# Moving every large on-chip tile of a hybrid decoder layer to a multiple of 512 bytes

## The chip, the core and the metric

The kernel runs on one core of one Trainium2 chip. Time is device time in microseconds (us) of one execution of the whole layer. The kernel before takes 894.34 us, the median of three runs (893.3 to 895.06).

## What is computed

One layer of a decoder trunk, 512 tokens of 1024 channels, in float32. The input is normed and projected (`z = u @ w_in`) into the inputs of three mixers: a chunked gated linear attention of 4 heads, a short gated convolution, and a sliding-window attention of 8 query and 2 key heads with sinks. Each mixer's output is projected back, the three are weighted by sigmoid gates and summed, and go through `w_o` into the residual. Then a second norm, a gated MLP, and a last norm:

```python
z = rmsnorm(h, g_mix) @ w_in                       # 1024 -> 7440 columns
merged = (gt[..., :D] * (o_gla @ w_gla_o) + gt[..., D:2*D] * (y_conv @ w_conv_o)
          + gt[..., 2*D:] * (o_swa @ w_swa_o))
h = h + merged @ w_o
hid = causal_dwconv(rmsnorm(h, g_ffn) @ w_up, ffn_conv_w)
h = h + (silu(hid[..., :2816]) * hid[..., 2816:]) @ w_down
out = rmsnorm(h, g_final)
```

## The kernel before

**Products.** Every large product is exact to about float32: each factor is split into two float32r parts, hi and lo, and three products are summed in one bank of PSUM: hi by hi, hi by lo, lo by hi. `by_channel` (line 173) holds a tile of weights still (128 columns of `whi` or `wlo`) and streams 512 tokens of an activation (`uh`, `ul`, or the outputs of the mixers) past it; its products are line 177. `by_token` (line 181) does the reverse: it holds 128 tokens of an activation still and streams 512 columns of weights past them; its products are lines 183, 184 and 186. Each product loads its still operand anew (PEld in the profile); the product itself (PE) is 512 columns wide, or 256 in two places where only half of the tokens are ready.

**Stages.** Input norm and first queries (to about 22 us), queries, keys, gates and the factors of the linear attention (to about 100 us), values, window attention and convolution (to about 245 us), the output gate `gr`, by `by_token`, the branch gates `gt` and output projections `ya`, `yb` of the three mixers, by `by_channel` (to about 470 us), the output projection `wo`, by `by_token` (to about 515 us), the MLP's up projection `ug`, `uu`, by `by_channel` (to about 764 us), and its down projection `wd`, by `by_token` (to the end).

**Side work.** The class `W` (line 52) streams weight blocks: while the products of one block run, ScalarE and VectorE split the next (lines 91 and 92), and SyncE loads the one after it (line 68). The small stages of the mixers are generators in a list `side`; `tick()` (line 107) takes one step of each after every 12 products. A scheduler then orders each engine's instructions. None of this is touched by the change.

**Where tiles lie.** A tile takes the same bytes of all 128 partitions. Pools are laid one behind the other from the low end in the order in which they are opened, or from the high end where `side="right"` is given; each tile is rounded up to 32 bytes. Line 43 opens `pc` (constants), line 44 `pw` (the weight blocks: three `raw`, two `whi`, two `wlo`, 8192 bytes each), line 45 `ph` (the four residual tiles `h`, 4096 bytes each), line 47 `small` (four of each of some thirty tiles of 4 to 32 bytes). `pU` (`uh` and `ul`, 16384 bytes each, later `uh2` and `ul2` in the same place) is opened behind `small`. The 45 slots of 2048 bytes (`pS`, line 249) grow from the high end, and after the output projection `pF` takes their place there (`xh`, `xl`, `yg`, `yu`, `p`). The constants end at byte 23840, which is 288 past a multiple of 512, so that the weight blocks and `h` lie 288 past one; the small tiles then put `uh` and `ul` at 416 past one; and the slots, counted from the high end, at 480 past one. All three are 32 past a multiple of 64. Tiles within a pool are multiples of 512 bytes apart, and the pieces of them that products read start at multiples of 512 bytes within the tile.

Of the kernel before, what the change touches and what calls it, by code (L numbers as in the profile page):

```python
# [7 lines left out]
F32 = mybir.dt.float32  # L8
# [6 lines left out]
P = 128  # L15
# [8 lines left out]
EPS = 1e-6  # L24
TAU = 16.0
NCONST = 6 * P
NSLOT = 45  # scratch tiles of [128, 512] up to the output projection
HEAD_STEPS = 3  # steps from the start of one linear-attention head to that of the next
LAG_STEPS = 5  # steps that a head's products wait for their factors
WINDOW_STEPS = 5  # steps from one window's start to the next one's  # L30

GQ, GK, GV, GR, GA = 0, 512, 1024, 1536, 2048
CX, CB, CC = 2064, 2576, 3088
# [4 lines left out]
def trunk(ctx, tc, x, g_mix, w_in, w_alpha, b_alpha, norm_g, conv_w, sinks, w_gla, w_conv, w_swa,  # L38
# [2 lines left out]
    mm = nc.tensor.matmul  # L41

    pc = ctx.enter_context(tc.tile_pool(name="pc", bufs=1))
    pw = ctx.enter_context(tc.tile_pool(name="pw", bufs=2))
    ph = ctx.enter_context(tc.tile_pool(name="ph", bufs=1))
    ps = ctx.enter_context(tc.tile_pool(name="ps", bufs=8, space=bass.MemoryType.PSUM))
    small = ctx.enter_context(tc.tile_pool(name="small", bufs=4))

    def bank():
        return ps.tile([P, 512], F32, tag="b", name="bank")  # L50

    class W:
        """A stream of weight blocks of 2048 columns per partition, each split exactly into two
        float32r parts. While the products of block i run, block i + 1 is split, in pieces, and
        block i + 2 is loaded."""

        def __init__(self):
            self.todo, self.raw, self.done, self.pieces = [], [], [], []
# [45 lines left out]
    at = {}  # L104
    side = []

    def tick():
        """One step of whatever runs beside the large products."""
        w.piece()
        for task in list(side):  # L110
            if next(task, side) is side:
                side.remove(task)
# [29 lines left out]
    for j in range(4):  # L142
        for b in range(3):
# [14 lines left out]
            n=1024,  # L158
# [32 lines left out]
        nc.vector.tensor_sub(out=lo, in0=src, in1=hi.bitcast(F32))  # L191

    def rstd_of(ss, n, tag, log=False):
        """(ss / n + EPS) ** -0.5, refined by one Newton step."""
        shape = list(ss.shape)
        v = small.tile(shape, F32, tag=tag + "v", name="v")
        r = small.tile(shape, F32, tag=tag + "r", name="r")
        t = small.tile(shape, F32, tag=tag + "t", name="t")
        nc.vector.tensor_scalar(out=v, in0=ss, scalar1=1.0 / n, scalar2=EPS, op0=ALU.mult, op1=ALU.add)
        if log:  # L200
            nc.scalar.activation(out=t, in_=v, func=AF.Ln)
            nc.scalar.activation(out=r, in_=t, func=AF.Exp, scale=-0.5)
        else:
            nc.scalar.activation(out=t, in_=v, func=AF.Sqrt)
            nc.vector.reciprocal(out=r, in_=t)
        u = small.tile(shape, F32, tag=tag + "u", name="u")
        nc.vector.tensor_mul(out=u, in0=r, in1=r)
        nc.vector.tensor_mul(out=u, in0=u, in1=v)
        nc.vector.tensor_scalar(out=u, in0=u, scalar1=-0.5, scalar2=1.5, op0=ALU.mult, op1=ALU.add)
        nc.vector.tensor_mul(out=r, in0=r, in1=u)  # L210
        return r

    def rstd_1(ss, e, n, tag, log=False):
        """(ss / n + e[0]) ** -0.5 for one column, refined by one Newton step; e[1] is -e[0] / 2."""
        v = small.tile([P, 1], F32, tag=tag + "v", name="v")
        r = small.tile([P, 1], F32, tag=tag + "r", name="r")
        t = small.tile([P, 1], F32, tag=tag + "t", name="t")
        if log:
            nc.scalar.activation(out=t, in_=ss, func=AF.Ln, scale=1.0 / n, bias=e[0])
            rstd_1.last = nc.scalar.activation(out=r, in_=t, func=AF.Exp, scale=-0.5)  # L220
        else:
            nc.scalar.activation(out=t, in_=ss, func=AF.Sqrt, scale=1.0 / n, bias=e[0])
            nc.vector.reciprocal(out=r, in_=t)
        nc.vector.tensor_scalar(out=v, in0=ss, scalar1=-0.5 / n, scalar2=e[1], op0=ALU.mult, op1=ALU.add)
        nc.vector.tensor_scalar(out=v, in0=v, scalar1=r, scalar2=r, op0=ALU.mult, op1=ALU.mult)
        nc.vector.tensor_scalar(out=r, in0=v, scalar1=1.5, scalar2=r, op0=ALU.add, op1=ALU.mult)
        return r

    def rstd_part(ss, n, tag, engine=nc.vector):
        """The first part of a sum of squares, for rstd_1 of the rest."""  # L230
        e = small.tile([P, 2], F32, tag=tag + "e", name="e")
        engine.tensor_scalar(out=e[:, 0:1], in0=ss, scalar1=1.0 / n, scalar2=EPS, op0=ALU.mult, op1=ALU.add)
        engine.tensor_scalar_mul(e[:, 1:2], e[:, 0:1], -0.5)
        return e[:, 0:1], e[:, 1:2]

    # ---- the input and its norm
    zero = pc.tile([P, 256], F32, name="zero")
    nc.vector.memset(zero, 0.0)
    idle = bank()

    def warm(n):
        """Products of zeros, to hold the tensor engine's clock up until the input is there."""
        for _ in range(n):
            mm(idle[:, 0:256], zero[:, 0:P], zero, start=True, stop=True)

# [78 lines left out]
        return ul[:, k, :]  # L324

    def a_tile(name, j, n=slice(0, S), acc=None):
        """Tile j of the channels of a weight block, by token."""
        if name == "gq0":
            hi, lo = (a.rearrange("p (j k c) -> p j k c", j=2, c=P)[:, j] for a in w.take(at[name]))
        else:  # L330
            hi, lo = (a.rearrange("p (k j c) -> p j k c", j=2, c=P)[:, j] for a in w.take(at[name]))
        acc = acc or bank()
        by_channel(acc, lambda k: hi[:, k], lambda k: lo[:, k], uhk, ulk, n=n)
        return acc

    def b_tiles(name):
        """The four token tiles of 512 channels, each as it is ready."""
        accs = [bank() for _ in range(NT)]
        for i in range(2):
            hi, lo = (a.rearrange("p (k c) -> p k c", c=512) for a in w.take(at[f"{name}{i}"]))  # L340
            for t in range(NT):
                tok = slice(t * P, (t + 1) * P)
                by_token(accs[t], lambda k: uh[:, 4 * i + k, tok], lambda k: ul[:, 4 * i + k, tok],
                         lambda k: hi[:, k, :], lambda k: lo[:, k, :], 4, i == 0, i == 1)
                if i:
                    yield t, accs[t]

    # ---- linear attention: queries, keys and gates
    qs, ks = [None] * GH, [None] * GH

    def got_q(h, acc):
# [78 lines left out]
            la[h] = z  # L430

    def running_sums(y, n):
        """In place: the sums of the first 1, 2, .. n of every n columns."""
        s = 1
        while s < n:
            g = y.rearrange("p (g s) -> p g s", s=2 * s)
            nc.vector.tensor_add(out=g[:, :, 2 * s - 1], in0=g[:, :, 2 * s - 1], in1=g[:, :, s - 1])  # L437
            s *= 2
        s = n // 4
        while s:  # L440
            g = y.rearrange("p (n g s) -> p n g s", s=2 * s, g=n // (2 * s))
            nc.vector.tensor_add(out=g[:, :, 1:, s - 1], in0=g[:, :, 1:, s - 1], in1=g[:, :, :-1, 2 * s - 1])
            s //= 2

    # ---- linear attention: the factors of each head
    ATs, qIs, kTs, decs = [None] * GH, [None] * GH, [None] * GH, [None] * GH

    def factors(h):
# [89 lines left out]
        nc.scalar.copy(out=v, in_=acc)  # L538
        vs.append(v)

    # ---- linear attention: states and outputs
    Os = [None] * NT

    def normed(n, O):
# [44 lines left out]

    side.append(states())  # L590

    # ---- window attention
    lower, upper = slice(0, 64), slice(64, 128)
    sqs = []
    for t in range(4):
# [36 lines left out]
    def window(n):  # L632
# [15 lines left out]
            return sps  # L648

        def biased(pr, sps):  # L650
            """Each query's last 128 keys: those of its own block up to itself, the others of the block before."""
            for i in range(2):
                s = slot(name="sc")[:, 0:256].rearrange("p (g j) -> p g j", g=2)
                ps2 = sps[i].rearrange("p (g j) -> p g j", g=2)
# [48 lines left out]
        for kt in kts:  # L703
            for g in range(2):
                t = n - 1 + kt
                mm(ops[64 * g:64 * g + 64, :], sv[:, t * P + 64 * g:t * P + 64 * g + 64], pts[kt, g],  # L706
                   start=kt == kts[0], stop=kt == 1)
# [10 lines left out]
    side.append(values())  # L718
    side.append(windows())

    # ---- short convolution
    def conv3(acc, cwj, name):
        """Three causal taps over the tokens, from PSUM or SBUF."""
        y = slot2(name=name)
        nc.scalar.activation(out=y, in_=acc, func=AF.Copy, scale=cw[:, 2, cwj:cwj + 1])  # L725
        nc.vector.scalar_tensor_tensor(out=y[:, 1:], in0=acc[:, :S - 1], scalar=cw[:, 1, cwj:cwj + 1],  # L726
# [24 lines left out]
            och.append(hi)  # L751
            ocl.append(lo)

    # ---- linear attention: output gate
    ogh = [slot(F32R, name="ogh") for _ in range(4)]
    ogl = [slot(F32R, name="ogl") for _ in range(4)]

# [15 lines left out]
    for t, acc in b_tiles("gr"):  # L773
        side.append(gated(t, acc))

    # ---- the gated sum of the branches
    mh, ml = [], []
    for j in range(4):
        gts = []
# [29 lines left out]
    uh = pU.tile([P, KT, S], F32R, name="uh2")  # L809
    ul = pU.tile([P, KT, S], F32R, name="ul2")  # L810

    # ---- output projection, residual, norm
    gf = [slot(name="gf") for _ in range(2)]
    for i in range(2):
        nc.gpsimd.dma_start(out=gf[i], in_=g_ffn[None, 512 * i:512 * i + 512].to_broadcast([P, 512]))
# [47 lines left out]
                elif two:  # L863
                    h_split(t - 2, hn[t - 2])

    # ---- gated MLP with a convolution
    first3 = [("ug0", 0), ("ug0", 1), ("uu0", 0)]
    early = []
    for i, (name, j) in enumerate(first3):
# [19 lines left out]
    xs = [None] * len(DOWN)  # L889

    def split_prods(i):
        """The factors of block i, split a tile at each step."""
        k0, kt = DOWN[i]
        xs[i] = [[], []]
        for k in range(kt):
            for part, name in zip(xs[i], ("xh", "xl")):
                part.append(pF.tile([P, 512], F32R, tag="t", name=name, bufs=22))
            split(xs[i][0][k], xs[i][1][k], prods[k0 + k])
            yield
# [92 lines left out]
```

## Time and profile before

| | |
|---|---|
| median of the runs (lowest, highest) | 894.34 us (893.3, 895.06) |
| profiled execution, span from first to last instruction | 891.6 us |
| PE busy, share of the span, instructions | 879.0 us, 99%, 3976 |
| PEld busy | 705.9 us, 79%, 3976 |
| DVE busy | 475.2 us, 53%, 822 |
| ACT busy | 342.8 us, 38%, 607 |
| POOL busy | 59.1 us, 7%, 58 |
| DMA | 82.39 MB, mean 92 GB/s |

PE is TensorE's products, PEld its loads of the still operand, DVE is VectorE, ACT ScalarE, POOL GpSimd, SP SyncE. Products are pipelined, so that the busy time of one (some 390 ns) is longer than the time from its start to the next one's start, and a PE busy at 99% isn't yet PE at its peak. What tells its rate is how many products start in a stretch of time. [...] What lies outside the span makes the difference between 891.6 and 894.34 us.

### The profile page before, as it was taken

Reading aid. Unit: us, or ns where it says so; the run is one execution under the profiler, and the core shown is the slowest. Engines: PE = TensorE matmul, PEld = TensorE weight load, DVE = VectorE, ACT = ScalarE, POOL = GpSimd, SP = SyncE. Lnnn points to the kernel's source line nnn. Section 1 sums busy time; section 2 is a strip of 40 time slices with the busy share of each in tenths; the row PEclk is TensorE's granted clock in tenths of the full one; section 3 lists DMA queues with packets and bytes.
Section 4 is the critical chain, followed back from the end, with each engine's and each line's share of the span. In section 5 each row is a group of like instructions: output and inputs, shape, how many; then the busy total and the mean of one; then the engine's idle time right before and its main releaser. Section 6 shows DMA issues by size and latency. Waiting matters only on the chain.

```text
span 891.6 us, 10006 instructions
## 1 busy us (share of the span) xinstructions
PE 879.0 (99%) x3976; PEld 705.9 (79%) x3976; DVE 475.2 (53%) x822; ACT 342.8 (38%) x607; POOL 59.1 (7%) x58
## 2 busy tenths in 40 slices
PE   8999999999999999999999999999999999999996
PEld 6887887767678888888888898888888888888885
DVE  5599566765633251526234666555555555743734
ACT  6545543443434132322223444333333333532533
POOL 2027003000000000101010000000000000001100
PEclk9999999999999999999999999999999999999999
DMA  9431331211222333233325134222222223222202
GB/s 278 145 94 48 95 95 48 86 56 48 78 66 71 95 93 115 77 95 96 87 79 165 48 118 139 93 92 93 94 92 93 92 69 113 96 71 95 95 1 94
DMA packets 69862, 82.39 MB, mean 92 GB/s; under 512 B 2875, under 2 KB 58455, under 8 KB 69815
## 3 DMA queue, kind: packets, MB, share of 16 engines
q1 hardware_dynamic: 69511, 80.70, 28.4%
q0 software_dynamic: 304, 1.05, 0.4%
q8 instruction: 31, 0.51, 0.2%
q14 instruction: 16, 0.13, 0.0%
HBM read 79.64 MB, written 2.10 MB: 92 GB/s over the span
## 4 chain that ended last, share of the span: by engine, by line
PE 92%; DVE 4%; ACT 1%; POOL 1%; issue 0%; DMA 0%; ACTq 0%
PE bank L177 64%; PE bank L184 7%; PE bank L183 7%; PE bank L186 7%; PE bank L647 1%; PE bank L706 1%; PE bank L646 1%; DVE wlo L92 1%; POOL d L461 1%; DVE z L437 1%; DVE d L479 0%; PE bank L693 0%; PE bank L566 0%; DMA h<-in_x 0%; ACT xsq L299 0%
## 5 line engine op out<-in xcount | busy, mean ns | idle before, releaser
L177 PE MATMUL bank<-uh,whi 128*128 128x512 f32 (+1 forms) x792 | 302.7, 386 | 1.9 <-ACT uh L315 1.6
L177 PE MATMUL bank<-ul,whi 128*128 128x512 f32 (+1 forms) x792 | 303.1, 386 | 0.2
L92 DVE TENSOR_TENSOR wlo<-raw,whi 128x1024 fp32r<-128x1024 f32 x144 | 176.5, 1259 | 196.1 <-ACT whi L91 113.0
L91 ACT CAST whi<-raw 128x1024 fp32r<-128x1024 f32 x144 | 144.4, 1048 | 174.6 <-PE bank L177 145.8
L177 PE MATMUL bank<-uh,wlo 128*128 128x512 f32 (+1 forms) x792 | 192.8, 384 | 0.0
L177 PEld LDWEIGHTS bank<-uh,whi 128*128 128x128 f32 x792 | 149.4, 189 | 35.5 <-ACT uh L315 2.1
L177 PEld LDWEIGHTS bank<-ul,whi 128*128 128x128 f32 x792 | 149.8, 189 | 33.4 <-issue 0.8
L177 PEld LDWEIGHTS bank<-uh,wlo 128*128 128x128 f32 x792 | 144.0, 188 | 32.3 <-issue 0.8
L184 PE MATMUL bank<-whi,xl 128*128 128x512 f32 x176 | 68.8, 392 | 0.0
L183 PE MATMUL bank<-whi,xh 128*128 128x512 f32 x176 | 67.9, 391 | 0.0
L186 PE MATMUL bank<-wlo,xh 128*128 128x512 f32 x176 | 48.0, 391 | 0.0
L191 DVE TENSOR_TENSOR xl<-p,xh 128x512 fp32r<-128x512 f32 x44 | 30.2, 726 | 26.9 <-ACT xh L190 22.6
L183 PEld LDWEIGHTS bank<-whi,xh 128*128 128x128 f32 x176 | 33.1, 188 | 7.3
L186 PEld LDWEIGHTS bank<-wlo,xh 128*128 128x128 f32 x176 | 33.1, 188 | 7.2
L184 PEld LDWEIGHTS bank<-whi,xl 128*128 128x128 f32 x176 | 33.1, 188 | 7.1
L190 ACT CAST xh<-p 128x512 fp32r<-128x512 f32 x44 | 24.7, 616 | 36.3 <-PE bank L184 36.3
L725 ACT ACTIVATE yg<-bank,cw 128x512 f32<-128x512 f32 x22 | 15.1, 685 | 53.3 <-PE bank L177 53.3
L797 DVE TENSOR_TENSOR g<-bank,g 128x512 f32<-128x512 f32 x24 | 16.5, 689 | 32.0 <-PE bank L177 31.4
L800 POOL TENSOR_TENSOR g<-g 128x512 f32<-128x512 f32 x8 | 13.4, 1673 | 302.7 <-DVE g L797 300.7
L784 ACT ACTIVATE g<-bank 128x512 f32<-128x512 f32 x24 | 14.3, 596 | 48.2 <-PE bank L177 48.1
L907 ACT ACTIVATE yg<-yg 128x512 f32<-128x512 f32 x22 | 13.9, 631 | 47.9 <-DVE yg L728 47.9
L726 DVE SCALAR_TENSOR_TENSOR yu<-bank,cw,yu 128x511 f32<-128x511 f32 x22 | 16.4, 747 | 26.4 <-ACT yu L725 26.4
(211 smaller groups left out, 963.1 us busy)
## 6 DMA issues: line engine op xcount, KB each, us to landing
raw<-in_w_in SPq DMA_DIRECT2D x28, 1024.0 KB, 5.2
raw<-in_w_up SPq DMA_DIRECT2D x22, 1024.0 KB, 5.1
raw<-in_w_down SPq DMA_DIRECT2D x10, 1024.0 KB, 5.0
raw<-in_w_o SPq DMA_DIRECT2D x4, 1024.0 KB, 5.0
h<-in_x SPq DMA_DIRECT2D x4, 512.0 KB, 4.8
raw<-in_w_gla_o SPq DMA_DIRECT2D x4, 512.0 KB, 3.4
raw<-in_w_conv_o SPq DMA_DIRECT2D x4, 512.0 KB, 4.6
raw<-in_w_swa_o SPq DMA_DIRECT2D x8, 256.0 KB, 4.1
```

The source lines that it names most:

```text
L91: nc.scalar.copy(out=hi[:, c], in_=raw[:, c])
L92: nc.vector.tensor_sub(out=lo[:, c], in0=raw[:, c], in1=hi[:, c].bitcast(F32))
L177: mm(acc[:, n], a, b[:, n], start=i == 0, stop=i == len(todo) - 1)
L183: mm(acc, xh(k), hi(k), start=start and k == 0, stop=False)
L184: mm(acc, xl(k), hi(k), start=False, stop=False)
L186: mm(acc, xh(k), lo(k), start=False, stop=stop and k == kt - 1)
L190: nc.scalar.copy(out=hi, in_=src)
L191: nc.vector.tensor_sub(out=lo, in0=src, in1=hi.bitcast(F32))
L725: nc.scalar.activation(out=y, in_=acc, func=AF.Copy, scale=cw[:, 2, cwj:cwj + 1])
L726: nc.vector.scalar_tensor_tensor(out=y[:, 1:], in0=acc[:, :S - 1], scalar=cw[:, 1, cwj:cwj + 1], in1=y[:, 1:], op0=ALU.mult, op1=ALU.add)
L784: nc.scalar.activation(out=g, in_=acc, func=AF.Sigmoid)
L797: nc.vector.tensor_mul(out=g, in0=acc, in1=g)
```

## The change

The pool of small tiles is opened directly behind the constants, ahead of the weight blocks, and is followed by a padding tile of 96 bytes; at the high end a padding tile of 480 bytes is laid first. Comments and docstrings fall away, and six lines are added ahead of most of the code, so that a line of the kernel after has the number of the line before plus 6 (line 177 becomes 183).

```diff
+PAD_LEFT, PAD_RIGHT = 96, 480
...
     pc = ctx.enter_context(tc.tile_pool(name="pc", bufs=1))
+    small = ctx.enter_context(tc.tile_pool(name="small", bufs=4))
+
+    pad = ctx.enter_context(tc.tile_pool(name="pad", bufs=1))
+    pad.tile([P, PAD_LEFT // 4], F32, name="pad")
+    pad_r = ctx.enter_context(tc.tile_pool(name="pad_r", bufs=1, side="right"))
+    pad_r.tile([P, PAD_RIGHT // 4], F32, name="pad_r")
     pw = ctx.enter_context(tc.tile_pool(name="pw", bufs=2))
     ph = ctx.enter_context(tc.tile_pool(name="ph", bufs=1))
     ps = ctx.enter_context(tc.tile_pool(name="ps", bufs=8, space=bass.MemoryType.PSUM))
-    small = ctx.enter_context(tc.tile_pool(name="small", bufs=4))
```

In the built programs every engine has the same instructions in the same order, with the same shapes and the same waits, and each tile name falls on the same buffer of its pool. What differs is the first byte of the tiles:

| tiles | first byte before | past a multiple of 512 | first byte after | past a multiple of 512 |
|---|---|---|---|---|
| constants (`zero`, `cst`, `rows`, ...) | 16512 | 128 | 16512 | 128 |
| `small` | 97568 | 288 | 23840 | 288 |
| `raw`, `whi`, `wlo` | 23840 | 288 | 27136 | 0 |
| `h` | 81184 | 288 | 84480 | 0 |
| `uh`, `uh2` / `ul`, `ul2` | 100768 / 117152 | 416 | 100864 / 117248 | 0 |
| slots of `pS` and `pF` | 137184 | 480 | 136704 | 0 |

## Rows read from the trace of the kernel before

**Rows 1.** Busy time, share of the span and instructions, by engine

```profile
PE 879.0 (99%) x3976; PEld 705.9 (79%) x3976; DVE 475.2 (53%) x822; ACT 342.8 (38%) x607; POOL 59.1 (7%) x58
```

**Rows 2.** Chain that ended last: shares by engine

```profile
PE 92%; DVE 4%; ACT 1%; POOL 1%; issue 0%; DMA 0%; ACTq 0%
```

**Rows 3.** PE's own waits: us in total, times, longest us

```profile
PE bank L177 <- ACT uh L315: 1.6, 2, 1.4
PE bank L244 <- DVE zero L238: 1.2, 1, 1.2
```

**Rows 4.** Stretches: PE, PEld, DVE, ACT, POOL busy (x instructions), PEclk, DMA share, GB/s

```profile
251.00:265.00 14.00, 14.00 (x62) 11.37 (x61) 6.45 (x8) 5.08 (x6) 0.00 (x0) 1.00 0.24 76
320.00:348.00 28.00, 28.00 (x122) 22.74 (x121) 7.33 (x8) 7.39 (x10) 0.00 (x0) 1.00 0.34 102
470.00:505.00 35.00, 35.00 (x154) 28.73 (x154) 15.78 (x32) 10.96 (x21) 0.00 (x0) 1.00 0.38 126
540.00:760.00 220.00, 220.00 (x944) 177.02 (x943) 117.99 (x140) 76.36 (x100) 0.00 (x0) 1.00 0.28 94
768.00:882.00 114.00, 114.00 (x500) 93.58 (x499) 58.69 (x86) 45.63 (x72) 6.18 (x4) 1.00 0.22 78
```

**Rows 5.** PE in order of time: start us, us, engine line op tiles shapes

```profile
14.31 0.42 PE L177 MATMUL bank<-uh,whi 128*128 128x256 f32 x1
...
15.16 0.41 PE L177 MATMUL bank<-uh,whi 128*128 128x256 f32 x1
17.88 0.28 PE L177 MATMUL bank<-uh,whi 128*128 128x256 f32 x1
...
19.80 1.12 PE L177 MATMUL bank<-uh,wlo 128*128 128x256 f32 x8
```

**Rows 6.** The same view of three early stretches

```profile
14.20:15.40 1.20, 1.20 (x8) 1.20 (x8) 1.20 (x4) 1.20 (x6) 0.47 (x2) 0.50 1.19 169
17.80:20.70 2.90, 2.90 (x27) 2.90 (x26) 1.21 (x4) 0.00 (x0) 0.00 (x0) 1.00 1.05 339
22.00:100.00 78.00, 76.94 (x383) 62.41 (x384) 61.98 (x126) 42.88 (x82) 23.69 (x15) 1.00 0.31 96
```

**Rows 7.** Groups by line and shape: count, busy us, mean ns, idle before

```profile
L177 PE MATMUL bank<-uh,whi 128*128 128x512 f32 x712 | 282.4, 397 | 0.0
L184 PE MATMUL bank<-whi,xl 128*128 128x512 f32 x176 | 68.8, 392 | 0.0
L183 PE MATMUL bank<-whi,mh 128*128 128x512 f32 x64 | 25.3, 395 | 0.0
L177 PE MATMUL bank<-osh,whi 128*128 128x512 f32 x32 | 12.7, 396 | 0.0
L177 PE MATMUL bank<-ul,whi 128*128 128x256 f32 x80 | 21.0, 301 | 0.2
L177 PEld LDWEIGHTS bank<-ul,whi 128*128 128x128 f32 x792 | 149.8, 189 | 33.4 <-issue 0.8 <-DVE ul L316 0.8 <-DVE ul L191 0.2
```

**Rows 8.** Line 177 by stretch: PE busy (x), PEld busy (x), PEclk, DMA

```profile
100.00:250.00 150.00, 103.00 (x419) 76.85 (x417) 1.00 0.23 71
250.00:480.00 230.00, 202.03 (x864) 162.29 (x864) 1.00 0.31 94
525.00:764.00 239.00, 238.43 (x1056) 193.08 (x1056) 1.00 0.28 93
```

**Rows 9.** VectorE groups by line and shape

```profile
L728 DVE SCALAR_TENSOR_TENSOR yg<-bank,cw,yg 128x510 f32<-128x510 f32 x22 | 16.5, 749 | 0.7
L726 DVE SCALAR_TENSOR_TENSOR yg<-bank,cw,yg 128x511 f32<-128x511 f32 x22 | 16.4, 747 | 21.3 <-ACT yg L725 21.3
L828 DVE SCALAR_TENSOR_TENSOR hn<-h,r,gf 128x512 f32<-128x512 f32 x8 | 5.7, 748 | 0.1
```

**Rows 10.** Chain in order of time, its only DMA: start us, us, what

```profile
0.72 3.25 DMA h<-in_x
```

**Rows 11.** DMA issues: count, KB each, median us to landing

```profile
raw<-in_w_up SPq DMA_DIRECT2D x22, 1024.0 KB, 5.1
```

## The prediction, made before the kernel after was run

> **What bounds the kernel now.** I read the busy times first, then the chain, PE's waits, and last how many products start in a stretch. PE is busy 99% of the span while DVE has 53% and ACT 38% [rows 1], and the chain that ended last lies on PE for 92% [rows 2]; its longest waits are 1.6 and 1.2 us [rows 3]. So the time is the number of products times the time from one start to the next, plus some 22 us ahead and 7 us behind. Nothing is issued, waited for or loaded differently after the change. It can act only by making some access to on-chip memory faster or slower, and on PE that counts at once.
>
> The interval is found from a stretch with nothing else on PE. A product shows for 0.39 us [rows 7], so the products that touch a stretch of L us cover L + 0.39 us of starts. The up projection: 220.39 / 944 = 233.5 ns. The branch gates: 28.39 / 122 = 232.7. The output gate: 14.39 / 62 = 232.1. The output projection: 35.39 / 154 = 229.8. The down projection: 114.39 / 500 = 228.8 [rows 4]. One product too many or few makes 3.7 ns at the output gate, 1.5 at the output projection, 0.5 or less in the two longest. All have 512 columns, a fresh load of 128 columns and the full clock. The output gate and the two later `by_token` stages run the same code; they differ in the tile that is held still, which lies at 416 past a multiple of 512 in the first and at 480 in the others. Nor do the other engines explain it: DVE is busy 54% of the up and 51% of the down projection, DMA 28% and 22%, ACT 35% and 40% [rows 4], too alike for two rates. So the rate seems to hang on where the operands lie. This is the only sign in the trace that the change can do anything.
>
> How large can it be? At the half clock, 0.50 granted, four products of 256 columns take 15.16 - 14.31 = 0.85 us, 212.5 each [rows 5, 6]; by the ratio of the clocks 512 columns take 212.5 at the full one. There the interval is 228.8 to 233.5, so 16.3 to 21 ns of each are not columns. At the full clock 16 products of 256 columns take 19.80 - 17.88 = 1.92 us, 120.0 each [rows 5], against 233.1 (mean of gates and up projection) for 512 columns with the same tiles. If an interval is a fixed part and a part that grows with columns, the fixed part is 2 x 120.0 - 233.1 = 6.9 ns and the other 113.1 per 256 columns, some 6.9 above the bare columns.
>
> **The change part by part.** *Products.* Before, every operand of the long products begins 32 bytes past a multiple of 64. My estimate is that the fixed 6.9 ns is what an operand pays that begins inside a unit of the memory, one unit more than it fills; 6.9 ns is about the time of 16 columns (212.5 / 512 x 16 = 6.6), 64 bytes, which fits a start in the middle of such a unit. It is only an estimate: no warm product of the trace has both operands on a multiple of 64. With the tiles at 0 it goes, and the part that grows with columns stays. The count from 250 us on, where PE never idles: 864 of line 177 up to 480 us, 984 in the up projection (1,056 less 72 of 256 columns) [rows 8], 192 of the output projection, 528 of the down projection (three times 64 and 176) [rows 7], and some 66 of the output gate (to 265 us at 232 ns), 2,634 in all: x 6.9 = 18.2 us. The 144 short ones around 515 to 535 us give 1.0. Between 100 and 250 us 419 of line 177 [rows 8] and some 30 of the output gate run beside the attention's side work; I count half, 1.5 us. Before 100 us I count none: DVE is busy 61.98 of 78 us there [rows 6] and its results come late as it is. Sum 20.7 us: 891.6 - 20.7 = 870.9 in the profiled execution, and with the 2.7 us that the median lies above that span, 874 us.
>
> Bounds for one product: if the whole gap goes, 16.3 ns for the 720 of output and down projection and 20.6 for the other 2,616 of the 3,336 long ones (712, 176, 64 and 32 of each kind in rows 7, with their fellows), that is 11.7 + 53.9 = 65.6 us, down to 829. On the other side, the new position can cost one more such fixed part, 3,336 x 6.9 = 23 us, up to 917. I take the middle of the gain, since the fixed part is the row nearest to what a shift of the start can change.
>
> Against this speaks the half clock: the same tiles in the same place show no gap there at all, so the start inside a unit is not a cost that every product pays, only perhaps one that becomes visible when columns are taken twice as fast. [...]
>
> *Loads of the still operand.* They take 189 ns [rows 7] beside a product whose interval is 229 or more, and are hidden by it; only where they slow the product's own reading do they count, and that is in the intervals above.
>
> *VectorE and ScalarE.* Of the same operation, 512 elements from a tile's start take 748 ns, 511 from 4 bytes later 747, 510 from 8 bytes later 749 [rows 9]: the place costs nothing. From -2 to 2 ns on some 1,400 instructions off the path: 0.
>
> *DMA.* The chain holds one transfer, 3.25 us for the first rows of the input [rows 10]; the weight blocks land in 5.1 us [rows 11], and the 48 products of one in the up projection take 48 x 233.5 ns = 11.2 us. A fifth more or less on the first transfer would be 0.65 us either way; I take 0.
>
> *Padding tiles, small tiles.* No instruction touches the padding. The small tiles keep their residue of 288. 0.
>
> **The rivals.** *Nothing happens.* The difference between stages comes from which region or pair of tiles is read, not from the residue; these stay as they are, and the time stays 894.3 (892.5 to 896.1). For it: no gap at the half clock, VectorE's indifference. Against it: `by_token` at 232.1 and 228.8 with one code.
>
> *Slower: the two readers of TensorE collide.* Before, the streamed and the held operand never have the same residue (288 with 416, 480, or the reverse). After, both begin at 0. The best pair, streamed 288 and held 480, gives 228.8; the others some 233. If equal residues are like the worse pairs, output and down projection lose 233.5 - 228.8 = 4.7 ns on 720 products, 3.4 us, and the rest stays: 897.7. The end is 917 as above. It decides if starts in the down projection come no closer than 233 ns.
>
> *Small gain.* Only the pair matters, and equal residues are as good as the best one seen: 2,616 products gain 233.1 - 228.8 = 4.3, 11.2 us: 883.
>
> *Large gain.* More than half of the whole gap goes: below 862, with the end at 829. [...]
>
> **How the numbers follow.** Forecast (862 to 884) 0.34; large gain 0.08; small gain (884 to 892.5) 0.10; nothing 0.29; slower 0.19. A time within 0.2% of before, 892.5 to 896.1, is what a measurement of this kernel can't tell from no change. Faster is 0.34 + 0.08 + 0.10 = 0.52, same 0.29, slower 0.19. The range for 8 in 10 must reach from part of the large gain over no change to the small loss: 852 to 898, which leaves out some 0.05 below and 0.10 above. Cases of both signs hold much of this; the forecast's own range is 862 to 884.
>
> **What would show it.** In the profile after, the up projection's stretch should hold 220.39 / 0.2266 = 973 products instead of 944, the down projection's 114.39 / 0.2219 = 515 instead of 500, at the same clock; the product's own shown duration should shrink by about as much. The durations of VectorE and ScalarE groups and the landings of loads should stay within 1%. PE's waits before 100 us may grow by 1 to 2 us. I am wrong if the intervals stay (nothing happens), if only the former 233 ns stages move (the pair matters, not the start), if the down projection slows, or if the time moves while the intervals of the long products don't.

## The result, and the profile after

The changed kernel takes 877.77 us (median of 4 runs, 877.42 to 878.00) beside 894.00 us of the kernel before on the same chip (893.30 to 895.06): a ratio of 0.982, interval 0.981 to 0.983. The profiled execution took 878.0 us, its span 876.2. The forecast was 874 us. The direction and most of the size came out; the reason that I gave for them did not, and that is what the experiments are about.

TensorE (PE) is still what bounds the kernel. The page's busy times, the answer to [rows 1]:

```profile
PE 862.9 (98%) x3976; PEld 705.2 (80%) x3976; DVE 474.2 (54%) x822; ACT 343.2 (39%) x607; POOL 59.4 (7%) x58
```

The counts are those of before. PE lost 16.1 us of busy time; the loads, VectorE and ScalarE kept theirs to 1 us. So the instructions of one engine became shorter, and that engine is the path.

Four stretches of the kernel after, in the columns of [rows 4] (branch gates, output projection, up and down projection; all stages begin earlier now, so the stretches differ a little):

```profile
320.00:348.00 28.00, 28.00 (x126) 23.18 (x125) 5.63 (x5) 8.27 (x11) 0.00 (x0) 1.00 0.29 92
462.00:497.00 35.00, 35.00 (x156) 29.01 (x155) 16.13 (x31) 11.64 (x22) 0.00 (x0) 1.00 0.40 133
540.00:760.00 220.00, 220.00 (x973) 182.15 (x972) 123.89 (x148) 85.40 (x114) 0.00 (x0) 1.00 0.28 94
768.00:860.00 92.00, 92.00 (x408) 76.18 (x407) 43.96 (x64) 35.32 (x56) 6.16 (x4) 1.00 0.19 63
```

By the same count of starts, (length + 0.39) / products: branch gates 28.39 / 126 = 225.3 ns (one product more or less is 1.8), output projection 35.39 / 156 = 226.9, up 220.39 / 973 = 226.5, down 92.39 / 408 = 226.4. Before they were 232.7, 229.8, 233.5 and 228.8. The two rates have become one, at the same granted clock (PEclk, a share of full speed) of 1.00. (The last 49 products in the up projection's stretch and the last 6 in that of the branch gates belong already to the stage behind.) Counted from start to start inside the output gate, it is 226.7 (below). A product's shown duration fell less, from 397 to 393 ns for `uh` with `whi` and from 392 to 389 for `whi` with `xl` (before in [rows 7]). The output gate, PE in order of time (start, length, line, operation, output <- streamed, held, shapes):

```profile
255.10 0.39 PE L189 MATMUL bank<-whi,uh 128*128 128x512 f32 x1
...
257.82 0.39 PE L189 MATMUL bank<-whi,uh 128*128 128x512 f32 x1
```

From 255.10 to 257.82 lie 12 starts: 2.72 / 12 = 226.7 ns.

The short products did not gain. The same 16 starts as in [rows 5], of 256 columns at the full clock:

```profile
18.03 0.28 PE L183 MATMUL bank<-uh,whi 128*128 128x256 f32 x1
...
19.95 1.12 PE L183 MATMUL bank<-uh,wlo 128*128 128x256 f32 x8
```

19.95 - 18.03 = 1.92 us, 120.0 ns each, what they took before. The 144 short ones between the output and the up projection even lost. The same 48 of them, in the kernel before (first two lines) and after:

```profile
526.31 0.28 PE L177 MATMUL bank<-uh,whi 128*128 128x256 f32 x1
...
532.01 0.28 PE L177 MATMUL bank<-uh,whi 128*128 128x256 f32 x1
518.59 0.28 PE L183 MATMUL bank<-uh,whi 128*128 128x256 f32 x1
...
524.35 0.28 PE L183 MATMUL bank<-uh,whi 128*128 128x256 f32 x1
```

5.70 / 48 = 118.8 ns before, 5.76 / 48 = 120.0 after.

What else the change could have touched stayed: VectorE's groups, the answer to [rows 9], each within 1 ns:

```profile
L734 DVE SCALAR_TENSOR_TENSOR yg<-bank,cw,yg 128x510 f32<-128x510 f32 x22 | 16.5, 748 | 0.7
...
L732 DVE SCALAR_TENSOR_TENSOR yg<-bank,cw,yg 128x511 f32<-128x511 f32 x22 | 16.4, 747 | 19.7 <-ACT yg L731 19.7
```

The chain's only transfer, the answer to [rows 10] (3.25 us there):

```profile
0.72 3.37 DMA h<-in_x
```

And the weight blocks of the up projection, with the median time to landing last, the answer to [rows 11] (5.1 us there):

```profile
raw<-in_w_up SPq DMA_DIRECT2D x22, 1024.0 KB, 5.0
```

PE's own longest waits (us in total, times, longest), with [rows 3]:

```profile
PE bank L183 <- ACT uh L321: 1.6, 2, 1.4
PE bank L315 <- DVE xn L309: 1.2, 2, 0.6
```

The first is as before; the transposes' waits for `xn` summed to 1.1 us before, so nothing new stands on the path.

Where the 15.4 us of the span came from, by the start of the first product of each stage in the two traces:

| stage (first product to the next stage's) | before, us | after, us | change | forecast |
|---|---|---|---|---|
| up to the output gate | 238.50 | 236.67 | -1.83 | -1.5 |
| output gate, branch gates, branch outputs | 229.92 | 224.41 | -5.51 | -6.4 |
| output projection | 38.48 | 38.08 | -0.40 | -1.3 |
| transposes and short products | 17.47 | 17.50 | +0.03 | -1.0 |
| up projection | 238.90 | 232.45 | -6.45 | -6.8 |
| down projection | 120.64 | 119.46 | -1.18 | -3.6 |
| after the last product | 7.69 | 7.65 | -0.04 | 0 |

The output projection's row ends with the first transposes of the second norm: its last 24 products lie in the row below, and half of the 144 short products in that of the up projection. The forecast's column is its own count of products times 6.9 ns. It holds where the interval was 233 ns, is three times too large where it was 229, and has the wrong sign for the short products.

### The profile page after: what moved, and what is told of

It is laid out like the page before. It is cut to its first block, busy times and chain, and to the rows that moved or that the text cites. A ratio compares the mean times of both kernels' runs of the same rounds, so it can differ in the third digit from the quotient of the medians.

```text
span 876.2 us, 10006 instructions
## 1 busy us (share of the span) xinstructions
PE 862.9 (98%) x3976; PEld 705.2 (80%) x3976; DVE 474.2 (54%) x822; ACT 343.2 (39%) x607; POOL 59.4 (7%) x58
## 4 chain that ended last, share of the span: by engine, by line
PE 92%; DVE 4%; ACT 1%; POOL 1%; issue 0%; DMA 0%; ACTq 0%
PE bank L183 64%; PE bank L190 7%; PE bank L189 7%; PE bank L192 7%; PE bank L653 1%; PE bank L712 1%; PE bank L652 1%; DVE wlo L98 1%; POOL d L467 1%; DVE z L443 1%; DVE d L485 0%; PE bank L699 0%; PE bank L572 0%; DMA h<-in_x 0%; ACT xsq L305 0%
## 5 line engine op out<-in xcount | busy, mean ns | idle before, releaser
L183 PE MATMUL bank<-ul,whi 128*128 128x512 f32 (+1 forms) x792 | 298.7, 381 | 0.2
L183 PE MATMUL bank<-uh,wlo 128*128 128x512 f32 (+1 forms) x792 | 188.9, 379 | 0.0
```

The source lines that it names most:

```text
L183: mm(acc[:, n], a, b[:, n], start=i == 0, stop=i == len(todo) - 1)
```

## The experiments

The theories, with the letters that the expectations use. **A**, the one of the prediction: an operand pays that begins inside a 64-byte unit. **B**: what counts is how far the start of the streamed operand lies from that of the held one; where they are equal in the low part of the address, a product takes least. **B1** is B with a repetition after 256 bytes, which the second bench tests. **C**: only multiples of 512 bytes, or of some other number above 64, help. Of these, only B lets two tiles at a "bad" place run fast.

**All tiles at 64, and all at 32.** Two kernels, the changed one with other sizes of the two padding tiles.

```diff
-PAD_LEFT, PAD_RIGHT = 96, 480
+PAD_LEFT, PAD_RIGHT = 160, 416    # all tiles 64 past a multiple of 512
+PAD_LEFT, PAD_RIGHT = 128, 448    # all tiles 32 past a multiple of 512
```

> The kernel after with both padding tiles changed (160 and 416 bytes), so that every large tile lies 64 past a multiple of 512. Theory A (an operand that starts off a multiple of 64 bytes costs a unit): as after, 877.8 us, up and down projection at 226.7 ns. Theory B (equal residues of streamed and held operand are what helps): also 877.8. Theory C (only multiples of 512, or of some number above 64, help): up projection back at 230 to 234 ns, 885 to 895 us.

> The kernel after with padding tiles of 128 and 448 bytes: every large tile lies 32 past a multiple of 512, so all residues are equal and none is a multiple of 64. Theory A: the gain goes, 890 to 897 us, intervals 229 to 234 ns. Theory B: the gain stays, 877.8 us, 226.7 ns. Theory C: as A.

At 64: 877.71 us, ratio 0.983 (0.982 to 0.984). At 32: 878.58 us, 0.984 (0.983 to 0.986). Up and down projection of the kernel with all tiles at 32, in the columns of the stretches above:

```profile
540.00:760.00 220.00, 220.00 (x973) 182.21 (x972) 124.57 (x150) 85.24 (x113) 0.00 (x0) 1.00 0.29 94
768.00:860.00 92.00, 92.00 (x408) 76.20 (x407) 43.76 (x64) 35.98 (x58) 6.16 (x4) 1.00 0.19 63
```

The same counts as after, 973 and 408, though every operand now begins inside a 64-byte unit as before. A falls, and C with it: that a tile lies at a multiple of 512 brings nothing by itself.

**Before, everything 32 bytes further on.** The converse: all operands at multiples of 64 (streamed and held at 320, 448 and 0 past a multiple of 512), their differences as before.

```diff
+    pad.tile([P, 8], F32, name="pad")        # ahead of pw
+    pad_r.tile([P, 120], F32, name="pad_r")  # right side
```

> The kernel before with a tile of 32 bytes ahead of the weight blocks and one of 480 at the high end: weight blocks at 320, uh and ul at 448, slots at 0, so that every pair of residues differs by as much as before (the differences -128, 128, 192) but all are multiples of 64. Theory A: 877.8 us and 226.7 ns in every stage. Theory B: as before, 894 us, 233 ns in the up and 229 in the down projection. Theory C: 885 to 894 us.

893.29 us, ratio 1.000 (0.999 to 1.001). Up and down projection:

```profile
540.00:760.00 220.00, 220.00 (x944) 176.98 (x943) 117.68 (x139) 77.08 (x100) 0.00 (x0) 1.00 0.29 94
768.00:882.00 114.00, 114.00 (x500) 93.54 (x499) 58.99 (x86) 45.70 (x73) 6.17 (x4) 1.00 0.23 79
```

944 and 500 products, to the unit what [rows 4] hold. Moving both operands together changes nothing at either place.

**Products alone, by place.** Groups of 48 products of 512 columns, a fresh load each, other engines idle, at chosen places of the streamed and the held operand (bytes past a multiple of 512).

```
tiles "sa".. streamed, "ha".. held; per pair 48 times:
nc.tensor.matmul(acc, tiles[held], tiles[streamed], start=..., stop=...)
```

> Products alone: 48 of 512 columns for each of 20 pairs of places of a streamed and a held operand, and of 256 columns for four pairs; the rest of the layer is left out and the output holds the input. Theory A: 226.7 ns where both operands start at a multiple of 64, whatever their difference; 229 to 234 where one or both start 32 past one; more for the streamed operand than for the held one, since the held one's load has 40 ns to spare. Theory B: 226.7 where the residues are equal, also at 32 and 32. Theory C: 226.7 at 0 and 0 alone. At 256 columns 120 ns at every place, as in both kernels, would say that the cost is not one per product.

PE in order of time; the difference of two starts over 48 is the interval. `sa`, `sb`, `sc` lie at 0, 32, 64, `sj` at 16, `sk` at 4, `sd` at 128; `ha`, `hb`, `hc`, `hi` at 0, 32, 64, 16:

```profile
33.42 11.07 PE L54 MATMUL bank<-sa,ha 128*128 128x512 f32 x48
44.33 11.37 PE L54 MATMUL bank<-sb,ha 128*128 128x512 f32 x48
55.53 11.36 PE L54 MATMUL bank<-sa,hb 128*128 128x512 f32 x48
66.72 11.07 PE L54 MATMUL bank<-sb,hb 128*128 128x512 f32 x48
77.64 11.15 PE L54 MATMUL bank<-sc,ha 128*128 128x512 f32 x48
88.62 11.36 PE L54 MATMUL bank<-sa,hc 128*128 128x512 f32 x48
99.82 11.06 PE L54 MATMUL bank<-sc,hc 128*128 128x512 f32 x48
...
199.64 11.21 PE L54 MATMUL bank<-sj,hi 128*128 128x512 f32 x48
210.68 11.51 PE L54 MATMUL bank<-sk,ha 128*128 128x512 f32 x48
222.03 11.31 PE L54 MATMUL bank<-sd,ha 128*128 128x512 f32 x48
```

0 with 0: 10.91 / 48 = 227.3 ns. 32 with 0: 11.20 / 48 = 233.3, and 0 with 32 11.19 / 48 = 233.1. 32 with 32: 10.92 / 48 = 227.5. 64 with 0: 10.98 / 48 = 228.8, but 0 with 64: 11.20 / 48 = 233.3; the sign of the difference counts. 4 with 0 is the worst seen, 11.35 / 48 = 236.5. 64 with 64 and 256 with 256: 10.90 / 48 = 227.1. One pair is an exception: 16 with 16 gives 11.04 / 48 = 230.0, so below 32 bytes equality alone is not enough. The places of before came out here as they do in the kernel: 288 with 480 at 228.9 (output and down projection), 480 with 288 at 233.3 and 416 with 288 at 232.4 (branch outputs, up projection), within some 1 ns of the kernel's stages. The four pairs of 256 columns gave 119.8 (0 with 0) and 119.7 (32 with 32), and 117.9 and 118.3 where the two differ by 32.

**Products alone, all differences, and narrower ones.** Sixteen places of the streamed operand in steps of 32 bytes against one held at 0, a few against one held at 96 (`hb` here), then held operands of 64 and 32 columns, and 384 and 256 streamed columns.

> Products alone again (the rest of the layer is left out, the output holds the input): 48 of 512 columns at 16 differences of streamed less held operand, 0 to 480 by 32, held at 0; four with the held one at 96; then held operands of 64 and 32 columns, and streamed ones of 384 and 256, at differences 0, 32 and 64. Theory B1 (only the difference counts, and it repeats after 256): 226.7 at 0 and 256, 233.3 at 32 and 288, 228.9 at 64 and 320, 232.4 at 128 and 384, 233.3 at 192 and 448, and the four with 96 as their differences -96, 0, 64, 128 say. Theory B2 (only exact equality modulo 512 helps): 226.7 at 0 alone, 229 to 234 elsewhere. If the held operand's load gets in the way of the stream, a load of half or a quarter of the columns brings the interval down towards 213 to 216 ns at every difference; if the stream pays by itself, it stays at 226.7 to 233.

```profile
36.58 11.04 PE L51 MATMUL bank<-sa,ha 128*128 128x512 f32 x48
47.46 11.37 PE L51 MATMUL bank<-sb,ha 128*128 128x512 f32 x48
...
125.69 11.05 PE L51 MATMUL bank<-si,ha 128*128 128x512 f32 x48
136.58 11.37 PE L51 MATMUL bank<-sj,ha 128*128 128x512 f32 x48
...
226.05 11.04 PE L51 MATMUL bank<-sd,hb 128*128 128x512 f32 x48
236.93 11.17 PE L51 MATMUL bank<-sf,hb 128*128 128x512 f32 x48
...
325.60 8.49 PE L51 MATMUL bank<-sa,ha 128*128 128x384 f32 x48
333.93 8.48 PE L51 MATMUL bank<-sb,ha 128*128 128x384 f32 x48
342.25 8.48 PE L51 MATMUL bank<-sc,ha 128*128 128x384 f32 x48
350.57 5.91 PE L51 MATMUL bank<-sa,ha 128*128 128x256 f32 x48
356.32 5.82 PE L51 MATMUL bank<-sb,ha 128*128 128x256 f32 x48
```

`sa` (0) takes 10.88 / 48 = 226.7 ns, `si` (256) 10.89 / 48 = 226.9: equal again after 256 bytes. `sd` with `hb`, both at 96, the same. From the first to the last start of each group the sixteen differences give, from 0 on: 226.7, 233.4, 229.1, 233.6, 233.4, 234.1, 233.2, 233.2, and from 256 on the same eight, each within 0.1 ns. With 384 columns the place no longer matters at the three differences tried: (333.93 - 325.60) / 48 = 173.5, the next 173.3. With 256 the equal pair is even the slower one, (356.32 - 350.57) / 48 = 119.8 against 117.9 at differences 32 and 64. So the three lengths of an equal pair lie on one line, (226.7 - 119.8) / 256 = 0.418 ns per column and 12.9 ns beside the columns (at 384 columns 173.3 by the line, 173.5 counted), and what an unequal pair adds, 2 to 8 ns at multiples of 32, appeared at 512 columns alone. With a held operand of 64 columns the interval was 230.0, 231.0 and 228.3 ns at differences 0, 32 and 64, with one of 32 columns 231.7, 232.9 and 231.7: a smaller held operand does not help, and there equality did not either.

**Each half of the change.** In the kernel before, only the held and streamed `u` tiles moved (to 288, where the weights lie), and only the slots moved (to 288).

```diff
+    gap.tile([P, 96], F32, name="gap")       # ahead of pU: u at 288, slots stay at 480
```
```diff
+    pad_r.tile([P, 48], F32, name="pad_r")   # right side: slots at 288, u stays at 416
```

> The kernel before with a tile of 384 bytes ahead of uh and ul, so that these and the weight blocks both lie at 288; the slots stay at 480. Theory B1: the 2,300 or so products of activations uh, ul with weights (gates, up projection, queries to values, output gate) go to 226.7 ns and give 14 us, 879 to 881 us; the down projection stays at 228.9, the branch outputs at 233.3. Theory A (multiples of 64): no change, 893. If all large tiles have to agree: no change either.

> The kernel before with a tile of 192 bytes at the high end, so that the slots lie at 288 as the weight blocks do; uh and ul stay at 416. Theory B1: 288 products of the branch outputs gain 6.7 ns and 720 of the output and down projection 2.2 to 2.4, 3.6 us, 889 to 890.5 us; the up projection stays at 233.3. Theory A: no change, 893.

`u` alone: 882.05 us, ratio 0.988 (0.987 to 0.990). Slots alone: 890.53 us, 0.997 (0.996 to 0.998). Beside the kernel before on that chip (892.77 us) that is 10.7 and 2.2 us, less than the 14 and 3.6 that B1 forecast, and together 12.9 of the 14.5 to 16.2 us that equal places everywhere gave in these comparisons. Output, up and down projection with `u` alone:

```profile
465.00:500.00 35.00, 35.00 (x152) 28.35 (x151) 15.22 (x31) 10.74 (x20) 0.00 (x0) 1.00 0.37 122
540.00:740.00 200.00, 200.00 (x884) 165.61 (x883) 109.93 (x130) 72.89 (x95) 0.00 (x0) 1.00 0.29 95
768.00:860.00 92.00, 92.00 (x403) 75.49 (x403) 44.85 (x60) 35.43 (x55) 6.17 (x4) 1.00 0.19 63
```

and up and down projection with the slots alone:

```profile
540.00:740.00 200.00, 200.00 (x859) 160.91 (x858) 105.82 (x125) 69.61 (x89) 0.00 (x0) 1.00 0.28 92
768.00:860.00 92.00, 92.00 (x408) 76.17 (x407) 50.41 (x69) 38.96 (x62) 6.17 (x4) 1.00 0.24 80
```

With `u` at the weights' place the up projection runs at 200.39 / 884 = 226.7 ns and the down projection, whose held operands are slots, stays at 92.39 / 403 = 229.3; with the slots there it is the other way, 200.39 / 859 = 233.3 and 92.39 / 408 = 226.4. The up and the down projection each follow their own pair. The output projection in the first kernel does not: its tiles lie where they lay before, but it ran at 35.39 / 152 = 232.8 ns where [rows 4] give 229.8. From start to start inside it, 24 products took 5.60 us (465.86 to 471.46), 233.3 ns each; in the kernel before they took 5.49 us (471.19 to 476.68), 228.8 each. That is 0.7 us of what the two halves lack; the rest lies ahead of the output projection and is not explained. So an unequal pair has more than one rate, with the same code and its tiles at the same places, and which one a stage falls into no run here settles; the equal one, at multiples of 32 and with a held operand of 128 columns, ran at 226.4 to 227.5 ns in every long stretch and in every group of 48 of one such pair.

**Products that alternate between places.** Does a product suffer from its own held operand's place, or from that of the next, which is loaded while it streams (the loads fill 182.15 of the 220 us of the up projection in which PE never pauses; theory **O** for the own pair, **L** for the next load)? Pairs in alternation tell: on line 63 each product's own pair is equal (0 with 0, 32 with 32), on line 66 the next one's load has the streamed operand's place; lines 69 and 72 the same with 64; on 75 only the streamed tile alternates, on 78 only the held one. At the end bf16 operands, with `ba`, `bb`, `bc` at 0, 32 and 64, held at 0.

> Products alone (the rest of the layer is left out, the output holds the input), in six rows of 48 of 512 columns in which two products alternate. Line 63: streamed and held operand of one product both at 0, of the next both at 32. Line 66: streamed 0 with held 32, then streamed 32 with held 0. Lines 69 and 72 the same with 64 for 32. Line 75: only the streamed one alternates, line 78 only the held one. Theory L (what counts is the held operand of the next product, whose load runs beside this product's stream): line 63 at 233, line 66 at 226.7, line 69 between 228.9 and 233, line 72 at 226.7. Theory O (a product's own two operands count): lines 63 and 69 at 226.7, line 66 at 233, line 72 between 228.9 and 233. Both say about 230 for lines 75 and 78. Then bfloat16 operands of 512 and 256 columns, streamed at 0, 32, 64 (and 128) and held at 0: if half the bytes leave room, one interval at every place, near 216 ns.

The first product of each line, then bf16 groups:

```profile
34.68 0.40 PE L63 MATMUL bank<-sa,ha 128*128 128x512 f32 x1
...
45.82 0.39 PE L66 MATMUL bank<-sa,hb 128*128 128x512 f32 x1
...
56.86 0.39 PE L69 MATMUL bank<-sa,ha 128*128 128x512 f32 x1
...
67.99 0.39 PE L72 MATMUL bank<-sa,hc 128*128 128x512 f32 x1
...
79.11 0.39 PE L75 MATMUL bank<-sa,ha 128*128 128x512 f32 x1
...
90.22 0.40 PE L78 MATMUL bank<-sa,ha 128*128 128x512 f32 x1
...
111.87 10.52 PE L57 MATMUL bank<-bb,wa 128*128 128x512 bf16 x47
122.23 10.52 PE L57 MATMUL bank<-bc,wa 128*128 128x512 bf16 x47
```

Line 63: 11.14 / 48 = 232.1 ns. Line 66: 11.04 / 48 = 230.0. Line 69: 11.13 / 48 = 231.9. Line 72: 11.12 / 48 = 231.7. Line 75: 11.11 / 48 = 231.5. Line 78, from its first start to its last (101.26): 11.04 / 47 = 234.9. Both theories fail: none falls to 226.7, so neither the own nor the next pair alone decides (line 66 stands half-way between 226.7 and 233.3), and how the places act on each other stays open. That tiles change is not the reason: the kernel after alternates between `uh` and `ul` and between weight blocks at 226.7 ns, with no change of place. The bf16 groups have 48 starts in 122.23 - 111.87 = 10.36 us (one record is missing), 215.8 ns; the next two groups, at 64 and 128, take the same 10.36 us, and the group at 0 has 47 in 111.87 - 101.72 = 10.15 us, 216.0.

**Other equal and unequal places in the changed kernel.** A gap ahead of the `u` tiles and another right pad put `u` and slots 256 bytes, and then 160 bytes, past the weights' place.

```diff
+    gap.tile([P, 64], F32, name="gap")   # with PAD_RIGHT = 224: 256 apart
```
```diff
+    gap.tile([P, 40], F32, name="gap")   # with PAD_RIGHT = 320: 160 apart
```

> The kernel after with a tile of 256 bytes ahead of uh and ul and 224 bytes at the high end: weight blocks and h at 0, uh, ul and slots at 256. Theory B1 (difference modulo 256): as after, 877 to 878.5 us, every stage at 226.7 ns. If residues have to be equal modulo 512: 888 us or more.

> The kernel after with tiles of 160 bytes ahead of uh and ul and 320 at the high end: weight blocks at 0, uh, ul and slots at 160, so that the differences are 160 (where weights are held) and -160, that is 96 modulo 256 (where they are streamed). Theory B1 with the measured 234.3 and 233.6 ns of these: slower than before, by 2 us in the stages up to the branch outputs, 1 us in the up projection and 3.5 in the output and down projection, 898 to 901 us. If before is as slow as places can make it: 893.

256 apart: 877.66 us, ratio 0.982 (0.981 to 0.984), as after. 160 apart: 898.97 us, ratio 1.006 (1.004 to 1.008), slower than before, as B1 said. Up and down projection at 160:

```profile
540.00:760.00 220.00, 220.00 (x940) 176.87 (x940) 118.58 (x141) 78.09 (x101) 0.00 (x0) 1.00 0.29 94
768.00:882.00 114.00, 114.00 (x490) 91.74 (x489) 60.55 (x88) 47.53 (x77) 6.20 (x4) 1.00 0.21 70
```

220.39 / 940 = 234.5 and 114.39 / 490 = 233.4 ns; the differences above have 234.1 for 160 and 233.6 for 96, which is what a streamed weight at 0 against a slot at 160 amounts to in 256. One theory thus gives both signs of the whole kernel's time from a bench of products alone.

## Why the prediction was right in size and wrong in its reason

**What bounds the kernel.** Right: PE at 99% of the span was the path, so 16.1 us less of PE is 15.4 less of span. The sign that the place matters, two rates with one code, was real, and it came from how far apart the two operands' residues lie.

**Products: the step that failed.** "My estimate is that the fixed 6.9 ns is what an operand pays that begins inside a unit of the memory ..." At multiples of 32 no operand pays for its own start: all at 32 past gives the whole gain (878.58 us), all at multiples of 64 with the old differences gives none (893.29 us). In its place the runs show that a product of 512 columns takes 2 to 8 ns more when streamed and held operand begin at different multiples of 32 modulo 256 bytes (228.8 to 234.1 alone), and nothing more when these are equal (226.7). By that, stages at 233 fall to 226.7 and stages at 229 fall to 226.7 too; the estimate took 6.9 from both. Hence the up projection as forecast (226.6 forecast, 226.5 counted) and the down projection not (221.9 forecast, 226.4 counted, a third of the gain).

**The number 6.9 was right by accident.** It was 2 x 120.0 - 233.1, on the assumption that 256 and 512 columns lie on one line. After the change the same working gives 2 x 120.0 - 226.7 = 13.3, a "fixed part" that grew although every long product shrank. The second bench shows why: the fixed part of an equal pair is 12.9 ns there, much like the 13.3 of the kernel, and the unequal pair's 6.4 ns (233.1 - 226.7) is added at 512 columns only, so the two lengths stood under different rules. The working took that 6.4 off 13.3, and what was left happens to be about as large as what was taken off. It hung on the rows that were read, too: the short products from 526.31 us on, in the same trace, took 118.8 ns, and with these the working gives 4.5 ns and a sum of 13.5 us. The sign of it was in the result's short products as well: a gain of 1.0 us was forecast there, and they lost some 0.2.

**The rivals.** "Nothing happens" is out; the missing gap at the half clock that spoke for it was read from products of 256 columns, which gained nothing at the full clock either. "The two readers of TensorE collide" named the right pair of tiles and had the sign wrong: equal residues are the best place (226.7 ns). "Small gain: only the pair matters" was right that the pair decides, and its condition (an equal pair as good as the best seen, 228.8) was 2.1 ns too careful; with 226.7 in its sum, 2,616 products gain 6.4 and 720 gain 2.1, 18.3 us against the 15.4 measured; before 240 us some 670 of these products should give 4.3 us, and 1.8 arrived; why the rest did not is not shown. "Large gain" is out for these products: no long stretch and no group of an f32 pair of 512 columns came under 226.4. The bf16 products of the bench took 215.8 ns; the f32 products of this kernel keep 10.9 ns more at the best place. In the f32 products of 512 columns the place of the held tile alone moves the interval by 6 ns (streamed from 0: 227.3 ns with the held one at 0, 233.1 with it at 32).

**The other terms.** VectorE, ScalarE, DMA, padding and small tiles at 0: right, by the rows above. The half counted before 250 us: 1.5 forecast, 1.83 measured; the half was a guess. The loads, hidden: their 189 ns did not change, and it is the place of the held tile against that of the streamed one that counted (227.3 and 233.1 ns, above); the prediction left this open in half a sentence and then followed the other trail.

**Sum.** 20.7 us forecast, 15.4 in the span. Of the 5.3 missing, 2.4 are the down projection, 0.9 the output projection, 1.0 the short products, 0.9 the gates and branches.

## What to carry to other kernels

Where TensorE streams 512 columns of one f32 tile while it loads 128 of another, as here, choose the two tiles' starts together: equal modulo 256 bytes, at multiples of 32, at whichever place (226.4 to 227.5 ns here, against 228.8 to 234.5); an alignment of each tile by itself bought nothing here (893.29 us with all at multiples of 64), and products of 256 columns lost 1 to 2 ns by equal places (120.0 against 118.8, 119.8 against 117.9). Look for it in the profile by counting product starts over a long stretch of each stage: stages of one shape and clock with different intervals are the sign. And a fixed cost taken from two sizes is only as good as the evidence that one rule holds at both; a third size would have shown that it does not, and so would the same size read at a second place of the trace.

## What the runs showed of the hardware that was not expected

- The interval of f32 products of 512 columns depends on streamed minus held start, with a sign: alone, +64 gives 228.8 ns and -64 gives 233.3; it repeats after 256 bytes (0 and 256: 226.7 and 226.9).
- It does so at 512 columns and not at 384 (173.3 to 173.5 at three differences); at 256 the equal pair is the slower one, by 1.4 to 1.9 ns in the benches (119.8 against 117.9 to 118.3) and 1.2 in the kernel (120.0 against 118.8).
- An unequal pair has several rates (288 with 480: 228.9 alone, 228.8 and 233.3 in the output projection of two kernels); the equal ones at multiples of 32, with 128 columns held, lie at 226.4 to 227.5 in every long stretch and in every group of 48 of one such pair.
- Products in which a tile's place changes from one to the next run at 230.0 to 234.9 ns, even where each product's own pair is equal (232.1 and 231.9).
- bf16 products show none of it: 215.8 to 216.0 ns at four places.

Why the place matters, and why only in the longest of the three products, no run here settles.
